# The input of the last SSM quarter is loaded into the tile of a rotation table

## The chip, the cores and the metric

The kernel runs on one core of a Trainium2 chip. The metric is the device time of one execution in microseconds (us), lower is better. The engines of the core are TensorE (PE, matrix products; PEld is its weight load), VectorE (DVE), ScalarE (ACT), GpSimd (POOL) and SyncE (SP, which here only starts transfers, DMAs). Each engine works through its own queue of instructions in order, and waits on semaphores for the other engines and for DMAs.

## What is computed

One layer of a hybrid streaming encoder on 1024 tokens of width 1024, with 16 learned tokens ahead of them. A normed input feeds two mixers side by side, an attention with forgetting and a state-space model (SSM); their outputs are gated and added, projected, and followed by a convolutional feed-forward part. Cut to what matters here:

```python
xn = rmsnorm(h, norm_mix_g)
q, k, v, f_logit, u, gates = split(xn @ w_in)
y_a = forgetting_attention(q, k, v, f_logit) @ w_attn_out
z = gelu(s5(u, ...))                       # s5: x_t = lam_bar * x_{t-1} + B u_t;  y_t = Re(C x_t) + D u_t
zg = z @ w_glu
y_s = zg[..., :1024] * sigmoid(zg[..., 1024:])
g = sigmoid(gates)
h = h + (g[..., :1024] * y_a + g[..., 1024:] * y_s) @ w_o
h = h + conv_ffn(rmsnorm(h, norm_ffn_g))
out = rmsnorm(h, norm_final_g)
```

The SSM has 32 groups of 16 channels, each with 64 complex states.

## The kernel before, in words

**Products.** All large products are done in two parts of reduced precision: each operand is split in a high part (a cast, on ACT or POOL) and a low part (the rest, a subtraction, most on DVE by the helper at line 137, `split_lo`), and three products are added: high by high, low by high, high by low. Weights come in chunks through the pool `wstream` (tile `raw`, two buffers; `whi` and `wlo`, two each). PSUM is taken in banks of 512 columns: three buffers `mm`, one `po`, two `sp`, two `tp`. `mm` and `po` are handed out in turn, so a product's bank is needed again four products later.

**The SSM** (function `ssm`) goes by four quarters of 8 groups. Time is folded in chunks of 8, which leaves 130 chunks. The quarter's input, `u_d[q]` in DRAM, is loaded as the tile `U` (128 x 8 x 130 floats). A quarter q runs in three steps, written as the generator `chain(q)`:

1. the load of `U` (two buffers, so that of quarter 3 takes the place of that of quarter 1), then 16 small products of `U` by the table `Wi`, into `wr` and `wi` (lines 1930 to 1934)
2. the rotation on DVE: `wr` and `wi` times the rotation table (`rc`, `rs`), a scan over the chunks, and the rotation back, into the states `St` (helper line 1653, scans 1951 and 1952). The rotation table is built once for quarters 0 and 1 (`rotation(0)`, tile `pc` in the pool `ssmb`), and once for quarters 2 and 3 (`rotation(1)`, a tile under the tag `pd` in another pool)
3. products of `St` by `Gm` and of `U` by `Tm` (lines 1971 and 1973), the copy to `Y`, a GELU, and the store of `Y` to `y_d[q]` in DRAM.

So `U` is read twice, in step 1 and at the end of step 3. `Wi` is made by `input_tables(q)`, `Gm` and `Tm` by `output_tables(q)`: products into `Kt` (line 1893), copied by ACT (1895), then eight DMAs on SP from `Kt` to `Tm` (1903).

**Around the SSM.** In the same stretch PE has the products for the gates as its main work (`stage_gates`, 8 chunks of 72 products of 342 columns, lines 170 to 172); the SSM's small products are put between them. After the last quarter come the logits of the forget gate (`fg`, lines 537 to 544), the first q and k products (`project_qk(0)`, lines 600 to 610: three blocks for q, three for k, each evicted by casts on ACT and `split_lo` on DVE), and then the GLU, `z @ w_glu`.

**The input of the GLU.** `load_z` loads the four `y_d[m]` as tiles `zt` of 128 x 8 x 130 floats. Each is eight DMAs of 16 partitions (line 641; half of those of m = 3 are started by POOL, the others by SP). They are split in high and low part (`zh`, `zl`, line 646 and the helper), and combined by additions and subtractions into four forms `zf` (lines 661 to 664), which are split too (`z1h`, `z1l` and so on). The GLU is a product by seven half-size products instead of eight (`seven`, lines 232 to 246), so it needs these combinations of its operands. The `zt` tiles, and the GLU's tiles after them, lie in memory that the SSM's pools have given back; a tile that comes to lie where an older one lay waits for the last reader of the older one. The SP queue also carries the loads of the GLU's weights (`raw<-in_w_glu_dram`, line 678), two DMAs for a chunk, into the two `raw` buffers; a load waits until ACT has cast what was in the buffer before (line 154 for the weights of q and k).

**What sets the order.** The code is written step by step, but the order in which instructions stand in each engine's queue is set when the program is built, by the framework's scheduler, which goes by its own estimate of when operands and places are free. The queue is then fixed. The lines at which the quarters are stepped (before, line 566 on):

```python
    begin(1)
    for q in range(4):
        next(chains[q])                                 # step 2 of quarter q
        if q < 3:
            ssm_out(q + 1, sx if q == 1 else None)      # Gm, Tm of the next quarter
        advance(q)                                      # products of the gates
        run(chains[q])                                  # step 3
        if q < 2:
            begin(q + 2)                                # Wi, U, step 1 of quarter q + 2
```

Of the kernel before, what the change touches and what calls it, by code (L numbers as in the profile page):

```python
# [9 lines left out]
F = mybir.dt.float32  # L10
# [9 lines left out]
P = 128  # L20
# [18 lines left out]
NCH = L // CH  # L39
GQ = G // 4  # L40
# [18 lines left out]
def block_kernel(ctx, tc, x, meta, xbt, x0t, g1t, w_q, w_k, w_v, w_f, w_u, w_g, b_f, w_ao, lam_d, bw_d, cw_d,  # L59
# [5 lines left out]
    V, S, GP, PE, SY = nc.vector, nc.scalar, nc.gpsimd, nc.tensor, nc.sync  # L65
# [41 lines left out]
    u_d = dp.tile([SW // P, P, P // GC, NCH], F, name="u_d")  # L107
# [69 lines left out]
    def run(gen):  # L177
        for _ in gen:
            pass
# [113 lines left out]
    sp = ByTag(sb, Gm=sa, Tm=sa, **{tag: sc for tag in ("wr", "wi", "ta", "tb", "dt8", "pd")})  # L293
# [14 lines left out]
    ssm_log, ssm_outs, ssm_loads, ssm_steps = ssm(tc, after, sp, sio, st_ps, ident, u_d, y_d, lam_d, bw_d, cw_d, d_sk, l_dt)  # L308
# [28 lines left out]
    for i in range(5, 9):  # L337
        load_x(i)
    us2, ul2 = (sp.tile([P, 2, n, SW if n == 2 else NCH], dt, tag=tag, name=nm, bufs=1)
                for n, dt, tag, nm in ((CH, F, "pd", "usb"), (2, R, "pc", "ul")))  # L340
    ul = [sio.tile([P, 2, SW], R, tag="U", name="ul", bufs=2) for _ in range(2)] + [ul2[:, i] for i in range(2)]

# [114 lines left out]
        after(ld, queue[-1])  # L457
    next(ssm_steps)
    after(ssm_log[n_log], ready)
    ssm_in, ssm_out, ssm_chain = next(ssm_steps)  # L460


    chains = {}
# [1 line left out]
    def begin(q):  # L465
        ssm_in(q)
        chains[q] = ssm_chain(q)
        next(chains[q])
# [53 lines left out]
    def advance(q):  # L522
        while n_gate[0] < BEHIND[q]:
            next(gates)
            n_gate[0] += 1
# [41 lines left out]
    begin(1)  # L567
    for q in range(4):
        next(chains[q])
        if q < 3:  # L570
            ssm_out(q + 1, sx if q == 1 else None)
        advance(q)
        run(chains[q])
        if q < 2:
            begin(q + 2)
        if q == 1:
            next(ssm_steps)
# [682 lines left out]
    for p in (0, 4, 1, 5, 2, 3, 6):  # L1260
        if p == 2:
# [7 lines left out]
            early = {m: pair_weights(m) for m in (NFF, 0)}  # L1269
# [372 lines left out]
def ssm(tc, after, sp, sio, s_ps, ident, u_d, y_d, lam_d, bw_d, cw_d, d_sk, l_dt):  # L1642
    nc = tc.nc
    V, S, GP, PE, SY = nc.vector, nc.scalar, nc.gpsimd, nc.tensor, nc.sync
# [7 lines left out]
    def TT(*a):  # L1652
        log.append(V.tensor_tensor(*a))
# [4 lines left out]

    bufs = dict(Gm=2, Tm=2, Wi=2, U=2, tq=3, sy=3, wr=2, wi=2, dt8=1, ta=1, tb=1, pc=1, pd=1, dg=1)

    def big(tag, shape, name=None):
        return (sio if tag in ("sy", "U") else sp).tile(shape, F, tag=tag, name=name or tag, bufs=bufs[tag])

# [18 lines left out]
    def rest():  # L1682
# [140 lines left out]
        def rotation(h):  # L1823
            pc = big("pd" if h else "pc", [P, 2, NH, NCH], "pc")
            GP.memset(pc[:, 0, :, 0:1], 1.0)
            GP.memset(pc[:, 1, :, 0:1], 0.0)
            rt = big("sy", [P, 2, 2, NH * 32], "rt")
            m_ = 1
            while m_ < NCH:
                w_ = min(m_, NCH - m_)  # L1830
                lg = m_.bit_length() - 1
                nh = min(NH, NH * 32 // w_)
                t, u = (rt[:, i, :, :nh * w_].rearrange("p c (a w) -> p c a w", w=w_) for i in range(2))
                for a0 in range(0, NH, nh):
                    sl = slice(a0, a0 + nh)
                    br, bi = (eq[lg][:, i, NH * h + a0:NH * h + a0 + nh].unsqueeze(1).unsqueeze(3)
                              .broadcast_to([P, 2, nh, w_]) for i in range(2))
                    times(pc[:, :, sl, m_:m_ + w_], pc[:, :, sl, :w_], br, bi, t, u)
                m_ *= 2
            return pc[:, 0], pc[:, 1]  # L1840
# [65 lines left out]
        def input_tables(qt):  # L1906
# [11 lines left out]
                S.copy(Wi[:, 4 * q:4 * q + 4].rearrange("p g m -> p (g m)"), wt)  # L1918
            state[qt] = [Wi]

        def chain(qt):
            Wi, = state[qt]
            U = big("U", [P, GQ, NCH])
            (S if qt > 1 else SY).dma_start(U, u_d[qt])
            wr, wi = (big(n, [P, HQ, NCH]) for n in ("wr", "wi"))
            for e in range(2):
                for q in range(0, HQ, 2):
                    wps = s_ps()
                    for i in range(2):
                        PE.matmul(wps[:, NCH * i:NCH * i + NCH], Wi[:, 2 * (q + i) + e, :], U[:, 2 * (q + i) + e, :],  # L1930
                                  start=True, stop=True)
                    w3 = wps[:, :NCH * 2].rearrange("p (i n) -> p i n", n=NCH)
                    S.copy(wr[64 * e:64 * e + 64, q:q + 2], w3[:64])
                    S.copy(wi[64 * e:64 * e + 64, q:q + 2], w3[64:])
            yield
            dt8 = big("dt8", [P, HQ, NCH])
            S.copy(dt8, dec[:, qt * HQ:qt * HQ + HQ].unsqueeze(2).broadcast_to([P, HQ, NCH]))
            GP.memset(dt8[:, :, 0:1], 0.0)
            rc, rs = (t_[:, qt % 2 * HQ:qt % 2 * HQ + HQ] for t_ in rot[qt // 2])
            ta, tb = (big(n, [P, HQ, NCH]) for n in ("ta", "tb"))  # L1940
            TT(ta, wr, rc, ALU.mult)
            TT(tb, wi, rs, ALU.mult)
            TT(ta, ta, tb, ALU.add)
            TT(tb, wr, rs, ALU.mult)
            TT(wi, wi, rc, ALU.mult)
            TT(wi, wi, tb, ALU.subtract)

            def fl(t_):
                return t_.rearrange("p a n -> p (a n)")

            V.tensor_tensor_scan(fl(wr), fl(dt8), fl(ta), 0.0, ALU.mult, ALU.add)
            V.tensor_tensor_scan(fl(ta), fl(dt8), fl(wi), 0.0, ALU.mult, ALU.add)
            St = big("sy", [P, GQ, NCH], "St")
            V.memset(St[:, :, 0:1], 0.0)
            S4 = St.rearrange("p (a b) n -> p a b n", b=2)
            for part, (op, fa, fb) in enumerate(((ALU.subtract, wr, ta), (ALU.add, ta, wr))):
                x_, y_ = (tb, wi) if part == 0 else (ta, wr)
                TT(x_, rc, fa, ALU.mult)
                TT(y_, rs, fb, ALU.mult)
                for e in range(2):  # L1960
                    r_ = slice(64 * e, 64 * e + 64)
                    TT(S4[64 * part:64 * part + 64, :, e, 1:], x_[r_, :, :NCH - 1], y_[r_, :, :NCH - 1], op)
            yield
            _, Gm, Tm = state.pop(qt)
            Y = big("sy", [P, GQ, NCH], "Y")
            for q in range(0, GQ, 3):
                nq = min(3, GQ - q)
                yps = s_ps()
                for i in range(nq):
                    yo = yps[:, NCH * i:NCH * i + NCH]  # L1970
                    PE.matmul(yo, Gm[:, q + i, 1:, :].rearrange("p t c -> p (t c)"), St[:, q + i, :],
                              start=True, stop=False)
                    PE.matmul(yo, Tm[:, q + i, :], U[:, q + i, :], start=False, stop=True)
                S.copy(Y[:, q:q + nq].rearrange("p a n -> p (a n)"), yps[:, :NCH * nq])
            outs.append(S.activation(Y, Y, AF.Gelu_apprx_tanh))
            outs.append(GP.dma_start(y_d[qt], Y))

        yield input_tables, output_tables, chain
        rot.append(rotation(1))
        yield  # L1980

    return log, outs, loads, rest()


# [56 lines left out]
```

## Time and profile before

| | |
|---|---|
| time, median of 3 runs | 1444.85 us (1443.14 to 1447.14) |
| the profiled execution: time, span in the profile | 1444.9 us, 1443.1 us |
| busy over the span: PE, PEld | 1422.4 us (99%), 1346.8 us (93%) |
| busy: DVE, ACT, POOL | 1073.0 us (74%), 722.2 us (50%), 762.9 us (53%) |
| mean granted clock of PE | 0.998 |
| SSM quarters, first product of step 1 to last product of step 3 | 87.8 to 180.4 us |
| first product of the GLU | 211.0 us |

The page gives busy times of the engines over the whole span; the views by window, the groups by line, the waits and the timeline go into one stretch. In a timeline row stand the start, the duration, the engine, the line, the operation, out<-in and the shape, and in brackets how long the engine had been idle before it and what ended that. `SPq`, `ACTq` are DMAs started from the queues of SP and ACT. Matmuls overlap each other, so a row's duration is longer than the distance to the next. The time outside the span is 1444.9 less 1443.1, 1.8 us.

### The profile page before, as it was taken

The page shows a single profiled execution, that of the slowest core. Times are in us where ns is not written, and L with a number is a line of the kernel's source. Part 1 is how long each engine was busy: PE and PEld are TensorE (multiplying, and loading weights), DVE is VectorE, ACT ScalarE, POOL GpSimd, SP SyncE. Part 2 cuts the span into 40 slices and gives each one's busy share as a digit, 9 for nine tenths or more (in the row PEclk, how much of TensorE's full clock was granted, in tenths as well). Part 3 has the DMA queues.
Part 4 walks back from the last instruction along what each step waited for, and adds up shares of the span by engine and source line. Part 5 has one row for each costly group of instructions (what it writes and reads, how often), then busy time and mean ns, then how long its engine had stood idle before and what let it go on. Part 6 is the DMA issues. An engine that isn't in the chain of part 4 may idle for free.

```text
span 1443.1 us, 26612 instructions
## 1 busy us (share of the span) xinstructions
PE 1422.4 (99%) x9655; PEld 1346.8 (93%) x9655; DVE 1073.0 (74%) x2203; ACT 722.2 (50%) x1419; POOL 762.9 (53%) x887
## 2 busy tenths in 40 slices
PE   8999999999999999999999999999999999999997
PEld 8999999988999999999879999999999999888886
DVE  7999788843657676656469987788877876788857
ACT  7646585423656565533646544444434445644433
POOL 1542248632456556515871335555555545888794
PEclk9999999999999999999999999999999999999999
DMA  8676644530147422167964156667753327864433
GB/s 303 169 182 164 153 102 151 150 106 30 38 130 165 126 66 67 45 222 244 267 147 142 63 139 170 171 164 190 187 136 116 92 71 262 328 204 142 123 87 117
DMA packets 92968, 214.06 MB, mean 148 GB/s; under 512 B 15090, under 2 KB 22898, under 8 KB 92452
## 3 DMA queue, kind: packets, MB, share of 16 engines
q1 hardware_dynamic: 73124, 166.32, 35.2%
q0 software_dynamic: 17696, 41.29, 15.2%
q10 hardware_dynamic: 2016, 4.74, 0.9%
q8 instruction: 76, 1.25, 0.4%
q14 instruction: 56, 0.46, 0.1%
HBM read 170.88 MB, written 71.71 MB: 168 GB/s over the span
## 4 chain that ended last, share of the span: by engine, by line
PE 91%; DVE 5%; DMA 1%; ACT 1%; issue 1%; POOL 0%; SPq 0%; POOLq 0%; ACTq 0%; DVEq 0%
PE mm L172 5%; PE mm L170 5%; PE mm L171 5%; PE sp L232 4%; PE sp L233 4%; PE sp L234 4%; PE tp L232 3%; PE tp L233 3%; PE tp L234 3%; PE mm L232 3%; PE mm L234 3%; PE mm L233 3%; PE tp L860 3%; PE mm L1557 2%; PE mm L1555 2%; PE mm L1556 2%
## 5 line engine op out<-in xcount | busy, mean ns | idle before, releaser
L170 PE MATMUL mm<-xhi,whi 128*128 128x342 f32 (+2 forms) x480 | 156.8, 327 | 1.0 <-DVE q L137 1.0
L172 PE MATMUL mm<-xhi,wlo 128*128 128x342 f32 (+2 forms) x480 | 155.3, 324 | 0.0
L171 PE MATMUL mm<-xlo,whi 128*128 128x342 f32 (+2 forms) x480 | 155.2, 324 | 0.0
L1183 POOL TENSOR_TENSOR ov<-ov,og 128x1024 f32<-128x1024 f32 x21 | 50.8, 2421 | 117.1 <-ACT og L1182 114.7
L137 DVE TENSOR_TENSOR sw<-sf,sw 128x512 fp32r<-128x512 f32 x72 | 73.5, 1021 | 45.6 <-ACT sw L1174 45.3
L1174 ACT CAST sw<-sf 128x512 fp32r<-128x512 f32 x72 | 44.9, 623 | 111.3 <-POOL sf L1321 82.3
L170 PEld LDWEIGHTS mm<-xhi,whi 128*128 128x128 f32 x480 | 90.5, 188 | 2.1 <-PE sp L818 0.8
L172 PEld LDWEIGHTS mm<-xhi,wlo 128*128 128x128 f32 x480 | 90.2, 188 | 0.6 <-issue 0.2
L171 PEld LDWEIGHTS mm<-xlo,whi 128*128 128x128 f32 x480 | 90.4, 188 | 0.2
L867 ACT CAST th<-tp 128x256 fp32r<-128x256 f32 (+3 forms) x120 | 56.1, 471 | 62.5 <-PE tp L860 30.2
L137 DVE TENSOR_TENSOR tl<-tp,th 128x256 fp32r<-128x256 f32 (+3 forms) x120 | 65.2, 547 | 25.9 <-ACT th L867 24.5
L1321 POOL TENSOR_TENSOR sf<-raw,sf 128x512 f32<-128x512 f32 x36 | 63.5, 1764 | 38.7 <-DVE sw L137 38.6
L1321 POOL TENSOR_TENSOR sf<-raw 128x512 f32<-128x512 f32 x36 | 49.1, 1364 | 62.2 <-ACT sw L1174 22.2
L234 PE MATMUL mm<-xhi,sw 128*128 128x258 f32 (+1 forms) x288 | 81.0, 281 | 0.0
L232 PE MATMUL mm<-xhi,sw 128*128 128x258 f32 (+1 forms) x288 | 80.8, 281 | 0.0
L233 PE MATMUL mm<-xlo,sw 128*128 128x258 f32 (+1 forms) x288 | 80.7, 280 | 0.0
L832 POOL TENSOR_SCALAR pt<-pt,nm 128x144 f32<-128x144 f32 (+4 forms) x72 | 52.1, 736 | 49.9 <-DVE nm L831 48.9
L1373 DVE SCALAR_TENSOR_TENSOR ov<-hv,cwt,ov 128x1024 f32<-128x1024 f32 x36 | 68.5, 1904 | 0.4 <-ACT ov L1371 0.4
L1174 ACT CAST sw<-raw 128x512 fp32r<-128x512 f32 x70 | 43.0, 620 | 46.6 <-PE sp L234 22.6
L830 ACT ACTIVATE pt<-pt,nm 128x144 f32<-128x144 f32 (+4 forms) x72 | 52.9, 735 | 25.7 <-DVE nm L829 25.2
L137 DVE TENSOR_TENSOR sw<-raw,sw 128x512 fp32r<-128x512 f32 x70 | 58.3, 837 | 5.3 <-ACT sw L1174 5.1
L823 DVE CUSTOM_DVE_ANT_0 pt<-sp,fb 128x328 f32<-128x328 f32 (+8 forms) x112 | 46.4, 430 | 21.2 <-PE sp L818 12.6
(722 smaller groups left out, 5720.7 us busy)
## 6 DMA issues: line engine op xcount, KB each, us to landing
raw<-in_w_up_dram SPq DMA_DIRECT2D x44, 512.0 KB, 3.8
t_d<-in_w_dn_dram POOLq DMA_DIRECT2D x44, 256.0 KB, 6.7
wr<-t_d SPq DMA_DIRECT2D x44, 256.0 KB, 3.8
ar<-a_d SPq DMA_DIRECT2D x41, 256.0 KB, 5.2
a_d<-ov SPq DMA_DIRECT2D x18, 512.0 KB, 2.6
wr<-in_w_dn_dram SPq DMA_DIRECT2D x33, 256.0 KB, 4.0
t_d<-in_w_dn_dram SPq DMA_DIRECT2D x22, 256.0 KB, 4.7
t_d<-t_d SPq DMA_DIRECT2D x22, 256.0 KB, 4.6
```

The lines of the kernel that those rows point to most:

```text
L137: return eng.tensor_tensor(out_, src, hi.bitcast(F), ALU.subtract)
L170: yield PE.matmul(ps, whi[:, i, :], ahi[:, i], start=(i == 0), stop=False)
L171: yield PE.matmul(ps, whi[:, i, :], alo[:, i], start=False, stop=False)
L172: yield PE.matmul(ps, wlo[:, i, :], ahi[:, i], start=False, stop=(i == k - 1))
L232: PE.matmul(ps, a[0][:, i], bh, start=(i == 0 and not joins), stop=False, skip_group_check=True)
L233: PE.matmul(ps, a[0][:, i], bl, start=False, stop=False, skip_group_check=True)
L234: PE.matmul(ps, a[1][:, i], bh, start=False, stop=(i == kh - 1), skip_group_check=True)
L830: S.activation(pt[:n, :kc], pt[:n, :kc], AF.Exp, bias=nm[:n, 1:2], scale=0.125, accum_out=nm[:n, 2:3])
L867: S.copy(th[:kn, z:tw], tp[:kn, z:tw])
L1174: S.copy(hi, src)
L1321: sums.append(GP.tensor_tensor(f_, a, b, op))
L1373: V.scalar_tensor_tensor(out=o, in0=h_[:, j:SEQ + j], scalar=cwc(j, m), in1=o, op0=ALU.mult, op1=ALU.add)
```

## The change

The load of `U` is taken out of `chain` into a function of its own, `load_u`. For quarter 3 the tile is no longer a buffer of the tag `U`: it is allocated under the tag `pc`, in the place of the rotation table of quarters 0 and 1. And the load of quarter 3 is called earlier in the code, right behind step 2 of quarter 1 instead of at the start of step 1 of quarter 3. It is still started from the ACT queue. Nothing else in the text changes.

```diff
@@ the stepping of the quarters
     begin(1)
     for q in range(4):
         next(chains[q])
+        if q == 1:
+            ssm_u(3)
         if q < 3:
             ssm_out(q + 1, sx if q == 1 else None)
         advance(q)
@@ in ssm
+        early = {}
+
+        def load_u(qt):
+            U = sp.tile([P, GQ, NCH], F, tag="pc", name="U", bufs=1) if qt == 3 else big("U", [P, GQ, NCH])
+            (S if qt > 1 else SY).dma_start(U, u_d[qt])
+            early[qt] = U
+            return U
+
         def chain(qt):
             Wi, = state[qt]
-            U = big("U", [P, GQ, NCH])
-            (S if qt > 1 else SY).dma_start(U, u_d[qt])
+            U = early.pop(qt) if qt in early else load_u(qt)
             wr, wi = (big(n, [P, HQ, NCH]) for n in ("wr", "wi"))
...
-        yield input_tables, output_tables, chain
+        yield input_tables, output_tables, chain, load_u
```

(`ssm_u` is `load_u` as the stepping code names it.) Behind the inserted lines the line numbers of the changed kernel are higher by 2, and behind `load_u` by 9.

The scheduler makes a new order of it, and three places of it matter below. The first is the ACT queue around step 1 of quarter 2, whose copies are `wr` and `wi`, and step 3 of quarter 1, whose copies are `Y`. Before:

```order
L1933 COPY wr<-tp 64x260
L1934 COPY wi<-tp 64x260
L1933 COPY wr<-sp 64x260
L1934 COPY wi<-sp 64x260
L1895 COPY Kt<-tp 16x512
...
L1974 COPY Y<-tp 128x260
L1924 DMA U<-u_d 128x1040
L1975 ACT_TABLE_LOAD
```

and now:

```order
L1942 COPY wr<-tp 64x260
L1943 COPY wi<-tp 64x260
L1927 DMA U<-u_d 128x1040
L1942 COPY wr<-sp 64x260
L1943 COPY wi<-sp 64x260
L1897 COPY Kt<-tp 16x512
...
L1983 COPY Y<-tp 128x260
L1984 ACT_TABLE_LOAD
```

The load of quarter 3 stands ahead of the last two copies of step 1 of quarter 2, where it stood behind the last copy of `Y` of quarter 1.

The second place is the SP queue behind the last DMA to `Tm`. Before:

```order
L1903 DMA Tm<-Kt 16x8x16
L641 DMA zt<-y_d 16x8x130 x16
L678 DMA raw<-in_w_glu_dram 128x512 x2
L641 DMA zt<-y_d 16x8x130 x8
L678 DMA raw<-in_w_glu_dram 128x512 x2
L641 DMA zt<-y_d 16x8x130 x4
L675 DMA gl<-g_d 128x1026 x2
```

and now:

```order
L1905 DMA Tm<-Kt 16x8x16
L680 DMA raw<-in_w_glu_dram 128x512 x4
L643 DMA zt<-y_d 16x8x130 x28
L677 DMA gl<-g_d 128x1026 x2
L680 DMA raw<-in_w_glu_dram 128x512 x4
```

The weights of the first two GLU chunks stood behind the first 16 and behind 24 of the 28 loads of `zt`; now both pairs stand ahead of all 28.

The third place is the DVE queue while PE does the q and k products: `q` and `kl` are the evictions of these, `zl`, `z2l`, `z3l` and `zf` work on the GLU's input, `ops` on its weights, `fg` on the forget gate. Before:

```order
L663 TENSOR_TENSOR zf<-zt,zf 128x8x65
L137 TENSOR_TENSOR q_2517<-po,q_2517 64x272
L137 TENSOR_TENSOR q_2518<-po,q_2518 64x272
L664 TENSOR_TENSOR zf<-zt,zf 128x8x65
L137 TENSOR_TENSOR zl_2435<-zt,zh_2434 128x8x130
L549 SCALAR_TENSOR_TENSOR fg<-fg 40x520
L137 TENSOR_TENSOR z2l<-zf,z2h 128x520
L137 TENSOR_TENSOR z3l<-zf,z3h 128x520
L137 TENSOR_TENSOR zl_2433<-zf,zh_2432 128x520
L137 TENSOR_TENSOR q_2517<-mm,q_2517 64x384
L137 TENSOR_TENSOR q_2518<-mm,q_2518 64x384
```

and now, from the same place behind the first block of q:

```order
L665 TENSOR_TENSOR zf<-zt,zf 128x8x65
L666 TENSOR_TENSOR zf<-zt,zf 128x8x65
L137 TENSOR_TENSOR zl_2435<-zt,zh_2434 128x8x130
L137 TENSOR_TENSOR z2l<-zf,z2h 128x520
L137 TENSOR_TENSOR z3l<-zf,z3h 128x520
L137 TENSOR_TENSOR zl_2433<-zf,zh_2432 128x520
L663 TENSOR_TENSOR zf<-zt 128x8x65
L137 TENSOR_TENSOR q_2517<-mm,q_2517 64x384
L137 TENSOR_TENSOR q_2518<-mm,q_2518 64x384
L137 TENSOR_TENSOR zl_2435<-zt,zh_2434 128x8x130
L549 SCALAR_TENSOR_TENSOR fg<-fg 40x520
L665 TENSOR_TENSOR zf<-zt,zf 128x8x65
```

with these behind them:

```order
L137 TENSOR_TENSOR z1l<-zf,z1h 128x520
L137 TENSOR_TENSOR ops<-raw,ops 128x256
L137 TENSOR_TENSOR ops<-sf,ops 128x256
L137 TENSOR_TENSOR q_2517<-mm,q_2517 64x384
L137 TENSOR_TENSOR q_2518<-mm,q_2518 64x384
L137 TENSOR_TENSOR ops<-raw,ops 128x256
L137 TENSOR_TENSOR ops<-sf,ops 128x256
L137 TENSOR_TENSOR z3l<-zf,z3h 128x520
L666 TENSOR_TENSOR zf<-zt,zf 128x8x65
L137 TENSOR_TENSOR kl<-mm,k_2519 64x272
L137 TENSOR_TENSOR kl<-mm,k_2520 64x272
```

The first split of a `zt` into `zl` and most of the work on `zf` stood ahead of the evictions of q; now the work on the third and fourth `zt` stands between the evictions of the first, second and third block of q. The queues of POOL and ACT have the work on `zt` later in the same way. On PE one piece moves: the products of `U` by `Wi` of quarter 3, and those into `Kt`, stand 17 gate products earlier.

More of the change, by code (lines that the diff above doesn't have):

```diff
@@ L459, in block_kernel @@
     after(ssm_log[n_log], ready)
-    ssm_in, ssm_out, ssm_chain = next(ssm_steps)
+    ssm_in, ssm_out, ssm_chain, ssm_u = next(ssm_steps)
     chains = {}
```

## Prediction

> **What bounds the kernel now.** I read the page's first part first.
>
> ```profile
> PE 1422.4 (99%) x9655; PEld 1346.8 (93%) x9655; DVE 1073.0 (74%) x2203; ACT 722.2 (50%) x1419; POOL 762.9 (53%) x887
> ```
>
> PE is busy for 99% of the span, so an edit off PE gains only where it ends a wait of PE. The view of PE's waits shows what there is to gain.
>
> ```profile
> PE mm L351 <- ACT uh L409: 5.0, 1, 5.0
> ...
> PE sp L1930 <- DMA U<-u_d: 1.1, 1, 1.1
> ```
>
> The first row belongs to the start of the program. The second is the only wait that this edit can touch: step 1 of quarter 3 waits for its input. The chain of waits and PE's timeline show it in place (start, duration; in brackets the idle time before the row).
>
> ```profile
> 133.63 9.33 DMA U<-u_d
> ...
> 145.12 0.16 PE mm L170
> ```
>
> ```profile
> 143.10 0.68 PE L1930 MATMUL sp<-U,Wi 128*128 128x130 f32 x4 [1.11 <-DMA U<-u_d]
> ...
> 180.27 0.39 PE L1973 MATMUL tp<-U,Tm 128*128 128x130 f32 x2
> ```
>
> The transfer takes 9.33 us, and PE stands still for the last 1.11. The last product of `U` by `Tm`, the last reader of the tile, starts at 180.27; that matters below.
>
> **What is gained.** The old place of `U` is free long before 133.63, and only the instruction's position on ACT held the load back. In the new place it waits for the last read of `pc` by the rotation of quarter 1 on DVE, and ACT waits with it.
>
> ```profile
> 126.61 0.70 DVE L1653 TENSOR_TENSOR ta<-pc,ta 128x520 f32<-128x520 f32 x1
> ...
> 145.98 0.70 DVE L1653 TENSOR_TENSOR ta<-wr,pc 128x520 f32<-128x520 f32 x1
> ```
>
> ```profile
> 126.31 0.37 ACT L1933 COPY wr<-sp 64x260 f32<-64x260 f32 x1
> ...
> 128.51 0.57 ACT L1895 COPY Kt<-tp 16x512 f32<-16x512 f32 x1 [1.45 <-PE tp L1893]
> ```
>
> That read ends at 126.61 + 0.70 = 127.31. Without the DMA, the third copy of step 1 starts at 126.31, so ACT stands for about 1.0, then issues (0.4; SP's last row below has 1.75 / 4 = 0.44 for one). Behind it stand the two copies of 0.37 each, which end at 127.3 + 0.4 + 0.75 = 128.5 instead of 127.1, and then the copy of `Kt` at 128.51, which waited 1.45 for PE anyway. DVE reads what these copies write from 145.98. So the new wait costs nothing; without that cover it would cost PE up to 1.3.
>
> The load is then issued at 127.3 to 127.7 and, at 9.33, lands by 137.0. PE was free for it at 143.10 - 1.11 = 142.0, and now comes to it 17 gate products earlier, at 0.16 each (the second row of the chain): 142.0 - 2.7 = 139.3. The transfer would have to take 11.7 to be late. **Gain: 1.1 us**, and all of PE's later work comes 1.1 earlier.
>
> **What is lost.** In the old place nothing followed `U`. The new one lies where the `zt` tiles of m = 1 and m = 2 are put afterwards, so these two loads get a wait for the last `U` by `Tm` product of quarter 3 (180.27, now about 179.2). That wait itself is met in time, as the next numbers show. But the scheduler, going by its own estimates, turned the SP queue round for it: all four loads of GLU weights now stand ahead of all 28 loads of `zt`. This is what costs. SP before:
>
> ```profile
> 155.44 10.35 SPq L641 DMA_DIRECT2D zt<-y_d  x16
> 165.90 0.90 SPq L678 DMA_DIRECT2D raw<-in_w_glu_dram  x2
> ...
> 174.87 4.92 SPq L641 DMA_DIRECT2D zt<-y_d  x8
> 179.95 0.83 SPq L678 DMA_DIRECT2D raw<-in_w_glu_dram  x2
> ...
> 189.94 1.75 SPq L641 DMA_DIRECT2D zt<-y_d  x4
> ```
>
> Before, 16 loads of `zt` were started from 155.44. The second pair of `raw`, at 179.95, could not go earlier than its buffer came free, and that is by ACT's cast of the weights of k:
>
> ```profile
> 176.96 1.05 ACT L154 CAST whi<-raw 128x1024 fp32r<-128x1024 f32 x1 [0.88 <-PE po L171]
> ```
>
> It ends at 178.01, was waiting for PE (0.88), and so comes 1.1 earlier: 176.9. Now this wait stands ahead of every `zt`, and behind it on SP stand the 28 loads and then the loads of `gl`. With 0.90 for the pair the first `zt` starts at **177.8**, 22 us later than before. The wait for 179.2 falls on m = 1, whose turn comes after eight loads, at 177.8 + 8 x 0.65 = 183.0, so it costs nothing.
>
> 24 loads (m = 0, 1, 2) take 10.35 + 4.92 = 15.27, so the last of m = 2 is issued at 193.1. From issue to use:
>
> ```profile
> 182.46 1.27 DVE L663 TENSOR_TENSOR zf<-zt,zf 128x520 f32<-128x520 f32 x1 [6.15 <-DMA raw<-in_w_glu_dram]
> ...
> 186.48 1.83 DVE L137 TENSOR_TENSOR z2l<-zf,z2h 128x520 fp32r<-128x520 f32 x1
> ...
> 196.24 1.29 DVE L663 TENSOR_TENSOR zf<-zt,zf 128x520 f32<-128x520 f32 x1 [0.83 <-DMA zt<-y_d]
> ```
>
> ```profile
> 186.17 1.59 POOL L662 TENSOR_TENSOR zf<-zt 128x520 f32<-128x520 f32 x1
> 190.21 2.16 POOL L641 DMA_DIRECT2D zt<-y_d  x4 [2.45 <-DMA y_d<-Y]
> ...
> 196.35 2.38 POOL L662 TENSOR_TENSOR zf<-zt 128x520 f32<-128x520 f32 x1 [0.43 <-issue]
> ```
>
> The loads issued until 174.87 + 4.92 = 179.79 were used by DVE at 182.46, 2.67 later (the row names the weights, but no operand of it is one). The last four of SP, issued until 191.69, and of POOL, until 192.37, were used from 196.24: at most 4.5 and 3.9. I take 3.2, near the first. So the work on m = 2 begins at 193.1 + 3.2 = **196.3**. Before, that was the time of m = 3 (the rows at 182.46 and 186.48 are of m = 2); now DVE and ACT have both ahead of, and between, the evictions of q and k. The four loads of m = 3, 1.75 behind m = 2, are there before either engine comes to them. What DVE then has to do, and when PE needed the banks:
>
> ```profile
> 197.56 0.89 DVE L137 TENSOR_TENSOR q<-po,q 64x272 fp32r<-64x272 f32 x2
> 198.49 1.37 DVE L664 TENSOR_TENSOR zf<-zt,zf 128x520 f32<-128x520 f32 x1
> 199.75 2.39 DVE L137 TENSOR_TENSOR zl<-zt,zh 128x1040 fp32r<-128x1040 f32 x1
> ...
> 203.79 0.68 DVE L137 TENSOR_TENSOR zl<-zf,zh 128x520 fp32r<-128x520 f32 x1
> 204.49 1.12 DVE L137 TENSOR_TENSOR q<-mm,q 64x384 fp32r<-64x384 f32 x2
> 205.64 0.42 DVE L137 TENSOR_TENSOR ops<-raw,ops 128x256 fp32r<-128x256 f32 x1
> ...
> 208.36 0.89 DVE L137 TENSOR_TENSOR kl<-mm,k 64x272 fp32r<-64x272 f32 x2
> ```
>
> ```profile
> 206.76 0.34 PE L170 MATMUL mm<-xhi,whi 128*128 128x384 f32 x1
> ...
> 211.00 0.28 PE L232 MATMUL mm<-zh,ops 128*128 128x260 f32 x1
> ...
> 211.72 0.28 PE L232 MATMUL mm<-zh,ops 128*128 128x260 f32 x1
> ```
>
> From 196.24 to 204.49 ten instructions took 8.25; their durations add up to 1.29 + 0.89 + 1.37 + 2.39 + 4 x 0.68 = 8.66 (four small ones, the last at 203.79), since rows overlap. So I take 0.953 of a sum. By the order now, and by these rows:
>
> - From 196.3 to the eviction of the second block of q: two `zf` 1.29 + 1.37, `zl` 2.39, three splits 3 x 0.68, `zf` 1.27, the eviction 1.12: 9.48, by 0.953 9.0, done at 205.3. The third product block of k takes that bank, at 206.76 - 1.1 = 205.65. No stall, with 0.3 to spare.
> - To the eviction of the third block of q: `zl` 2.39, `fg` 0.68, `zf` 1.29, `z1l` 0.68, two `ops` 0.84, the eviction 1.12: 7.00 more, 15.7 in all, done at 212.0. The first product of the GLU needs that bank at 211.00 - 1.1 = 209.9. **Stall 2.1.**
> - To the eviction of the first block of k: two `ops` 0.84, `z3l` 0.68, `zf` 1.37, `kl` 0.89: 3.78 more, 19.3 in all, done at 215.6. The second bank of the GLU needs it at 211.72 - 1.1 + 2.1 = 212.7. **Stall 2.9.**
>
> ACT has the like in its own queue:
>
> ```profile
> 196.18 2.36 ACT L646 CAST zh<-zt 128x1040 fp32r<-128x1040 f32 x1 [3.08 <-DMA zt<-y_d]
> ...
> 199.88 0.63 ACT L668 CAST zh<-zf 128x520 fp32r<-128x520 f32 x1 [0.39 <-DVE zf L664]
> 200.54 0.48 ACT L600 CAST q<-mm 64x384 fp32r<-64x384 f32 x1
> ...
> 201.53 0.41 ACT L682 CAST ops<-raw 128x256 fp32r<-128x256 f32 x1
> ...
> 204.00 0.38 ACT L605 CAST k<-mm 64x272 fp32r<-64x272 f32 x1
> ...
> 215.04 0.65 ACT L241 COPY c<-mm 128x260 f32<-128x260 f32 x2
> ```
>
> ```profile
> 215.47 0.39 PE L232 MATMUL mm<-zh,ops 128*128 128x260 f32 x1
> ```
>
> From 196.3 to the casts of the first block of k stand two casts `zh` of a `zt` (2 x 2.36), five of a `zf` (5 x 0.63), four of q (4 x 0.48) and four `ops` (4 x 0.41): 11.4. From there to the copy `c` it was 215.04 - 204.00 = 11.04 without a pause that new work could fill, and two more casts of a `zf`, 0.63 each, now stand in it: 12.3. So `c` starts at 220.0. The product at 215.47 followed its start by 0.43: 220.45, against 215.47 - 1.1 + 2.1 + 2.9 = 219.35. **Stall 1.1.**
>
> Before, PE was idle ahead of none of these four products (no brackets). Behind them I see nothing on DVE, ACT or POOL by which PE could win time back, since PE has no waits there to give up; so a stall reaches the end whole.
>
> **The sum.** -1.1 + 2.1 + 2.9 + 1.1 = +5.0. On the profiled execution's 1444.9 (span 1443.1 and 1.8 around it) this is **1449.9 us**. That execution lies on the median of the runs, 1444.85, so nothing is to be shifted.
>
> **Bounds.** The start of the work on m = 2 is the unknown. Its early end: the loads go at the pace of the last four, 1.75 / 4 = 0.44, and are used 2.67 later: 177.8 + 10.5 + 2.7 = 191.0. Then DVE is in time everywhere (206.7 against 209.9, 210.3 against 210.6), ACT is late by 0.8, and the net is -0.3: 1444.6. Its late end: 16 loads at 0.647 as at 155.44, and 4.5: 197.8, 1.5 later, which gives stalls of 1.2, 2.4, 2.9 and 1.1, net +6.5: 1451.4. The other unknown is how DVE and POOL get on. At 186.48 DVE's `z2l` took 1.83 where its like took 0.68, while POOL ran a `zf` of 1.59 from 186.17. Two such additions of POOL, those for m = 2 and m = 3, now fall in DVE's busiest stretch; at 1.15 each this adds up to 2.3, so the upper end is 1453.7. I take none of it in the sum, since beside the like addition of POOL at 196.35 it was POOL that took longer (2.38), and DVE's rows from 196.24 on kept to within 0.1 of 1.27.
>
> [...]
>
> **The rivals.**
>
> - *The loads are quick and the work on `zt` stays hidden; only the wait of `U` goes.* For it: the four loads at 189.94 went at 0.44. Against it: the 24 ahead of them at 0.61 to 0.65, with the same size. It decides at 196.3 - 6.1 = 190.2, that is 24 loads at (190.2 - 2.7 - 177.8) / 24 = 0.40 each. Time 1444.9 - 1.1 = 1443.8; with 0.44 it is 1444.6. Chance 0.18.
> - *DVE and POOL block each other (as the row 186.48), and PE waits longer.* For it that row; against it the rows from 196.24 on, which kept their usual durations. Time 1449.9 + 2.3 = 1452.2, with late loads 1453.7 and above. Chance 0.13.
> - *The change doesn't do what it says:* the load of `U`, now beside other traffic, takes over 11.7, and PE waits as before. Against it: 9.33 with traffic of its own at 133.95. Then the losses stand without the gain: 1451.0. Chance 0.03.
>
> **How the numbers follow.** The forecast has 0.66, with 1444.6 to 1451.4 as its own range. A measurement of this kernel tells 0.3% from no change, 4.3 us: faster is below 1440.5, which no case reaches, since the gain is at most 1.1; I leave it 0.02. Slower is above 1449.2. The sum lies just above that; of the forecast I put a little over half there (0.35), with nearly all of the two heavier rivals (0.15): 0.50, and 0.48 for no change. The range goes from the first rival, 1443.6, to 1454.0, beyond the upper bound.
>
> **What would show it.** Right: PE's row of waits for `U` is gone, and the load's start is near 127.5; ACT waits there for a read of `pc`; SP starts the first `zt` near 178 behind `raw`; the first `zf` of m = 2 on DVE starts near 196; PE waits before the first GLU products for DVE's `q` and `kl`, then for ACT's `c`, 2 to 3 us each. Wrong: the work on m = 2 begins before 192, or PE's waits between 205 and 221 add up to less than 3 us, or waits of a microsecond follow in the later chunks of the GLU, which I have at nothing.

## The result, and the profile after

The changed kernel takes 1453.03 us (median of 6 runs, 1451.53 to 1456.66), the kernel before 1444.65 (6 runs, 1443.14 to 1447.14): a ratio of 1.006, with a 95% interval of 1.0047 to 1.0073. It is 8.4 us slower, where 5.0 were forecast. The profiled execution of the changed kernel is the longest of its six (span 1454.9).

PE's waits between 100 and 300 us, where the change lies (line waited for: us in total, times, longest):

```profile
PE mm L170 <- DVE q L137: 3.5, 1, 3.5
PE mm L232 <- DVE kl L137: 2.9, 1, 2.9
```

The wait for `U` is gone. In its place stand two waits for evictions by DVE, 3.5 for the second block of q and 2.9 for the first block of k.

The gain first. ACT and PE around the early load, from the timeline:

```profile
126.85 0.33 ACTq L1927 DMA_DIRECT2D U<-u_d  x1
127.22 0.37 ACT L1942 COPY wr<-sp 64x260 f32<-64x260 f32 x1 [1.42 <-DVE ta L1655]
...
128.02 0.57 ACT L1897 COPY Kt<-tp 16x512 f32<-16x512 f32 x1
```

```profile
138.68 0.61 PE L1939 MATMUL sp<-U,Wi 128*128 128x130 f32 x4
```

ACT stands 1.42 for the last read of `pc`, as foreseen, and the copy of `Kt` takes the delay up: it has no idle time left before it. `U` is issued at 126.85, and PE comes to it at 138.68 without a wait.

Then the loss. SP, and DVE and POOL behind it:

```profile
161.28 15.68 SPq L680 DMA_DIRECT2D raw<-in_w_glu_dram  x4
177.08 18.50 SPq L643 DMA_DIRECT2D zt<-y_d  x28
```

```profile
198.47 1.31 DVE L665 TENSOR_TENSOR zf<-zt,zf 128x520 f32<-128x520 f32 x1 [4.12 <-DMA zt<-y_d]
199.82 2.30 DVE L666 TENSOR_TENSOR zf<-zt,zf 128x520 f32<-128x520 f32 x1
...
207.25 1.12 DVE L137 TENSOR_TENSOR q<-mm,q 64x384 fp32r<-64x384 f32 x2
...
217.52 0.89 DVE L137 TENSOR_TENSOR kl<-mm,k 64x272 fp32r<-64x272 f32 x2
```

```profile
198.63 2.31 POOL L664 TENSOR_TENSOR zf<-zt 128x520 f32<-128x520 f32 x1 [6.28 <-DMA zt<-y_d]
```

The row of `raw` spans the wait of its second pair; the first `zt` goes at 177.08. The work on m = 2 begins at 198.47, where 196.3 was forecast. The second `zf` on DVE takes 2.30 beside POOL's of 2.31; before it took 1.37. So the evictions come at 207.25 and 217.52, and PE behind them:

```profile
208.52 0.48 PE L170 MATMUL mm<-xhi,whi 128*128 128x384 f32 x1 [3.47 <-DVE q L137]
...
214.70 0.36 PE L232 MATMUL mm<-zh,ops 128*128 128x260 f32 x1 [0.19 <-DVE q L137]
...
218.56 0.36 PE L232 MATMUL mm<-zh,ops 128*128 128x260 f32 x1 [2.90 <-DVE kl L137]
```

These are the products that began at 206.76, 211.00 and 211.72 before. PE was ready for the first of them at 208.52 - 3.47 = 205.05, which is 1.7 earlier than before: so large is the gain where the first wait begins. 1.1 of it is the wait for `U`. Another 0.5 was there already at the first product of `U` by `Tm`, in quarter 0 (110.5 against 111.0), ahead of the new load; a wait of 0.3 for DVE between 100 and 110 is part of it, which the changed kernel's profile doesn't have. Whether the change brings that part isn't shown. Waits of 6.6 less a gain of 1.7 make 4.9, and the kernel lost 8.4. The rest is in the view of windows. Its columns are the stretch, its length, the busy time of PE, PEld, DVE, ACT and POOL (instructions in brackets), and then the granted clock of PE; the stretches are steps of 3.41 us counted from the changes of that clock (208.68, 212.09, 218.92 and 222.33):

```profile
205.27:208.68 3.41, 0.16 (x1) 0.19 (x2) 3.33 (x6) 1.76 (x5) 1.90 (x1) 1.00 0.00 0
208.68:212.09 3.41, 3.41 (x12) 3.41 (x12) 3.41 (x4) 3.31 (x9) 0.00 (x0) 0.50 0.47 154
212.09:215.51 3.42, 3.23 (x20) 2.88 (x18) 3.36 (x9) 3.35 (x6) 0.09 (x1) 0.99 0.00 0
215.51:218.92 3.41, 0.51 (x5) 0.39 (x4) 3.33 (x5) 3.36 (x6) 2.50 (x2) 1.00 0.08 14
218.92:222.33 3.41, 3.41 (x18) 3.41 (x18) 3.33 (x6) 3.35 (x9) 2.64 (x3) 0.50 0.42 144
```

Behind each of the two long waits, of 3.47 and 2.90, PE was granted half its clock (0.50) for 3.41 us. It did 12 products in 208.68 to 212.09, and 20, some of them smaller, in the next stretch. By an estimate from these rows, a clock of 0.50 for 3.41 us, each such stretch cost 3.41 / 2 = 1.7 us. The sum is 3.5 + 0.2 + 2.9 + 2 x 1.7 = 10.0, less the gain of 1.7: 8.3. The products of `wvh` by `xhi`, behind all of this, show the same (first and last start), before and after:

```profile
L754 PE MATMUL mm<-wvh,xhi x48: 387/393/497, 292.4 to 334.6; 128*128 128x512 f32 x48
```

```profile
L756 PE MATMUL mm<-wvh,xhi x48: 387/392/505, 301.1 to 343.3; 128*128 128x512 f32 x48
```

They start 8.7 us later, which agrees with the medians. The profiled execution is 11.8 longer in span. The rest, 3.1, belongs to a wait near 1320 and one more stretch of half clock behind it, 1.8 + 1.7 = 3.5:

```profile
PE sp L1557 <- DVE hs L1567: 1.8, 1, 1.8
```

```profile
1318.01:1321.43 3.42, 1.59 (x8) 1.24 (x7) 3.42 (x6) 2.28 (x4) 2.79 (x3) 1.00 0.45 152
1321.43:1324.84 3.41, 3.41 (x10) 2.63 (x9) 3.41 (x5) 0.00 (x0) 2.15 (x3) 0.50 0.43 146
```

A row of DVE ahead of it, at 1310.34, took 6.02 beside rows of POOL; in the kernel before no single row of that group took over 1.78 there. The prediction has no term for this wait. The profiles of three runs below have it too (1.7 or 1.8; the place alone, the order put back, the places exchanged), and the others don't. In the run with the place alone the clock behind it stayed at 1.00. Whether the change brings it isn't shown.

### The profile page after: what moved, and what is told of

Same layout as the page of the kernel before. It is cut to its first block, busy times and chain, and to the rows that moved or that the text cites. A ratio compares the mean times of both kernels' runs of the same rounds, so it can differ in the third digit from the quotient of the medians.

```text
span 1454.9 us, 26612 instructions
## 1 busy us (share of the span) xinstructions
PE 1427.7 (98%) x9655; PEld 1350.6 (93%) x9655; DVE 1069.8 (74%) x2203; ACT 722.3 (50%) x1419; POOL 758.9 (52%) x887
## 4 chain that ended last, share of the span: by engine, by line
PE 93%; DVE 2%; issue 2%; DMA 1%; ACT 1%; SPq 0%; POOL 0%; POOLq 0%; DVEq 0%; ACTq 0%
PE mm L170 5%; PE mm L172 5%; PE mm L171 5%; PE sp L233 4%; PE sp L232 4%; PE sp L234 4%; PE mm L232 3%; PE mm L234 3%; PE tp L232 3%; PE tp L233 3%; PE tp L234 3%; PE mm L233 3%; PE tp L862 3%; PE mm L1559 2%; PE mm L1558 2%; PE mm L1557 2%
```

## The experiments

The questions: do late data make the waits, or the new order of the queues, or the place of `U`? And is the half clock the price of any long wait of PE, or something of this place? Each new median stands beside one of the kernel before that was measured along with it. The diffs show the lines that matter, and some are written shorter than they are. Several expectations put the gain at 1.8, between the 1.7 above and the 1.9 by which the last product of `U` by `Tm` came earlier (178.5 against 180.4).

**The order of SP alone, on the kernel before.** `U` stays where and when it was.

```diff
         for q in range(2):
-            SY.dma_start(raw[:, 4 * q:4 * q + 4], w_glu[KD * q + i])
+            ld = SY.dma_start(raw[:, 4 * q:4 * q + 4], w_glu[KD * q + i])
+            for zl_ in zt_ld if i < 2 else []:      # all loads of zt
+                after(zl_, ld)
```

> The kernel before, U in its old place and loaded at its old time; only the SP queue is tied to the order of the changed kernel: all four loads of GLU weights ahead of the 28 loads of zt (DVE, ACT and POOL then get the work on zt late too). Theory (the late start of the zt loads costs, not the new place of U): no gain on U, so PE comes to the evictions 1.8 us later than in the changed kernel, and so do the weights of k and the loads; the work on m = 2 starts near 200.3, PE waits for DVE's q and kl for about 6.5 us in all, and half clock after the long waits costs 3.4 more: 1444.7 + 10 = 1454.7 (1452 to 1457). Rival (the place of U itself, by its waits on SP and ACT, costs): no loss here, 1444.7.

Measured: 1454.74 us against 1445.92, ratio 1.0067 (1.0052 to 1.0082). PE's waits:

```profile
PE mm L170 <- DVE q L137: 5.4, 1, 5.4
PE mm L232 <- ACT c L241: 1.4, 1, 1.4
PE mm L232 <- DVE kl L137: 0.9, 1, 0.9
```

The waits add up to 7.7, and behind the first the clock was 0.50 and 0.51 for two stretches (207.37 to 214.20), in the first of which PE was busy for 0.16 of 3.42 us. So the place of `U` as such isn't needed for the loss: it comes with late loads of `zt`, and the queues that go with them, in a kernel that keeps `U` where it was.

**The place alone.** The early call is taken back, the place kept.

```diff
         next(chains[q])
-        if q == 1:
-            ssm_u(3)
         if q < 3:
```

> The new place of U for quarter 3 alone; the call that loads it stands in the code where it stood before, at the start of step 1 of quarter 3. The scheduler makes the same queues of it as of the whole change. Theory (the place, not the line of the call, decides): the time of the changed kernel, 1453.0 (1451.5 to 1454.5), the load still started near 127. Rival (the early call matters): U lands late again, and PE's wait for it is back.

Measured: 1454.22 us against 1444.22, ratio 1.0062 (1.0047 to 1.0078).

```profile
126.83 0.33 ACTq L1925 DMA_DIRECT2D U<-u_d  x1
```

The load goes at 126.83 with the call where it was, and PE waits 4.0 for q and 2.8 for `kl`. The line of the call decides nothing here; the place gives both the early load and the loss.

**The order of SP put back, on the changed kernel.**

```diff
+            if i < 2:
+                after(ld, zt_ld[(15, 23)[i]])
+                for zl_ in zt_ld[(16, 24)[i]:]:
+                    after(zl_, ld)
```

> The changed kernel with the SP queue tied to the order of before (16 zt, 2 weights, 8 zt, 2 weights, 4 zt); U stays in the place of pc, so the loads of m = 1 and everything behind them on SP wait for the last product of U, near 179. DVE and ACT keep their late order of the work on zt, with small differences. Theory: m = 0 is loaded from 155, m = 1 from 179, m = 2 issued until about 190.5 and landed near 194 to 196 instead of 198.5, so the waits of PE shrink from 6.5 to 2 to 4 us, with one half-clock stretch or none: 1446 to 1450. Rival (order of the SP queue was the only cause): all of the loss goes, 1442.9.

Measured: 1453.22 us against 1445.92, ratio 1.0053 (1.0036 to 1.007): 7.3 us slower, where the changed kernel is 8.4, a difference within the intervals. The expectation failed, and so did its rival.

```profile
151.17 32.50 SPq L645 DMA_DIRECT2D zt<-y_d  x16
```

```profile
195.49 1.36 DVE L667 TENSOR_TENSOR zf<-zt,zf 128x520 f32<-128x520 f32 x1 [2.49 <-DMA zt<-y_d]
...
213.56 0.89 DVE L137 TENSOR_TENSOR kl<-mm,k 64x272 fp32r<-64x272 f32 x2
```

The work on m = 2 began 3.0 us earlier than in the changed kernel, and the wait for q went. But in this order more work on m = 3 stands ahead of `kl`: it came at 213.56, PE waited 4.3 for it and 0.9 for ACT's `c`, and had half clock for two stretches of 3.41 (0.51 and 0.50, 213.38 to 220.21).

**The places of m = 1 and m = 3 exchanged.** The same, with the tiles taken in the order 0, 3, 2, 1.

```diff
-        for m in range(4):
-            tag = "gl" if m % 2 else "ms"
-            zt = gz[tag].tile([P, CH, NCH], F, tag=tag, name="zt", bufs=2)
+        for m in (0, 3, 2, 1):
+            tag = "gl" if m % 2 else "ms"
+            places[m] = gz[tag].tile([P, CH, NCH], F, tag=tag, name="zt", bufs=2)
```

> As the run with the order of SP put back, and the tiles of zt of m = 1 and m = 3 exchange their places, so that only m = 2 and m = 3 lie over the new place of U. The loads of m = 0 and 1 go at 155, those of m = 2 at about 179 to 184.5, landed near 188. Theory (late data make the waits): DVE is in time for all evictions (188 + 19.3 = 207.3 against 209.2), no wait of PE, no half clock, and the gain of 1.8 is left: 1442.9. Rival (the order on DVE, with the work on zt between the evictions of q and k, costs by itself even when the data are there): PE waits of 2 us or more before the GLU, 1445 or above.

Measured: 1451.71 us against 1445.92, ratio 1.0048 (1.0033 to 1.0063). The edit did not do what it was meant to: the loads of m = 1 still waited, since the 16 loads span as long as above:

```profile
151.24 32.46 SPq L648 DMA_DIRECT2D zt<-y_d  x16
```

So this run repeats the one before it and tells nothing of the question.

**Early data, late order.** The pools are laid in another order, so that only m = 2 (and `zf`) lies over `U`; SP is tied as above.

```diff
-    gz = {n: pool(st_k2, "gated" + n, side="left") for n in ("ms", "gl", "cg")}
+    gz = {n: pool(st_k2, "gated" + n, side="left") for n in ("ms", "cg", "gl")}
```

> U stays in the place of pc as in the changed kernel. The pools of the gated tiles are laid in another order, so that only the zt of m = 2 (and zf) lie over U, and the SP queue is tied to the order of before. The loads of m = 0 and 1 go from 151, those of m = 2 from 179. DVE, ACT and POOL keep the late order that they have in the run with the order of SP put back (work on zt between the evictions of q and k). Theory (late data make the waits, the order alone does not): work on m = 2 can begin near 189 to 190, PE waits for less than 1 us, no half clock: 1443 to 1444. Rival (the order on DVE and ACT costs by itself): PE waits 2 us or more in front of the GLU, with half clock behind it: 1446 or above.

Measured: 1448.35 us against 1444.96, ratio 1.0017 (1.0007 to 1.0027). Here the edit did what it was meant to: m = 1 no longer waits for `U`, and the loads of m = 2 begin at 178.67.

```profile
150.73 12.19 SPq L645 DMA_DIRECT2D zt<-y_d  x16
```

```profile
190.96 2.12 DVE L667 TENSOR_TENSOR zf<-zt,zf 128x520 f32<-128x520 f32 x1
...
206.50 0.72 DVE L549 SCALAR_TENSOR_TENSOR fg<-fg 40x520 f32<-40x520 f32 x1
```

```profile
PE tp L232 <- ACT ops L690: 2.1, 1, 2.1
```

```profile
207.30 1.28 ACT L552 ACT_TABLE_LOAD   x1 [2.02 <-DVE fg L549]
```

With the work on m = 2 begun 7.5 us earlier (190.96 against 198.47) DVE is in time for q and, but for 0.2, for `kl`. So that part of the loss is late data. But the order costs too: the forget gate's step at 206.50 (201.96 before) stands on DVE behind the work on m = 3, ACT stood 2.02 for it, and `ops` behind it on ACT came late. PE waited 2.1, again with half clock (0.50) behind, here for two stretches:

```profile
215.32:218.73 3.41, 2.97 (x13) 2.63 (x13) 3.33 (x5) 3.30 (x10) 2.88 (x4) 0.50 0.58 191
218.73:222.15 3.42, 3.42 (x17) 3.42 (x17) 2.51 (x6) 1.43 (x6) 2.48 (x5) 0.50 0.44 154
222.15:225.56 3.41, 3.41 (x31) 3.41 (x30) 2.98 (x7) 2.09 (x4) 1.86 (x3) 1.00 0.04 5
```

**The price of a wait.** Far from the change, DVE multiplies a tile by 1.0 in place, as often as `HOLD` says, ahead of an eviction.

```diff
+        for _ in range(HOLD.get(n_seven[0], 0)):
+            hold = V.tensor_scalar(bot[:, last], bot[:, last], 1.0, None, ALU.mult)
         for q in st:
-            add(bot[:, q["l"]], prod(q, "b", None, A22, T4), q["c1"])
+            ev = add(bot[:, q["l"]], prod(q, "b", None, A22, T4), q["c1"])
+            if hold is not None:
+                after(ev, hold)
```

> The kernel before with PE made to wait in the feed-forward products, far from the change: in six of the 16 doubled blocks DVE gets 12, 16, 20, 24, 28 and 32 extra products by 1.0 in place, ahead of an eviction that PE needs. Theory: each wait of PE of about 3 us or more is followed by a stretch of 3.4 us at half the granted clock, which costs PE 1.7 us more; waits under 1 us are followed by none. Rival (the half clock in the changed kernel came from something else at that place, such as its other engines or DMAs): the clock stays at 1.00 through waits of any length.

> As the run with extra products on DVE in the feed-forward part, but fewer of them: 6, 7, 8, 9, 10, 10 and 11 in seven of the doubled blocks, for waits of PE of some 0.5 to 2.5 us. Theory, from the run before this: the clock is set for stretches of 3.41 us by the stretch before; where PE stood still for more than about half of a stretch (1.7 us or more that fall into one), the next is at half clock, so waits under 1.4 bring none and waits of 2 and more bring one where they fall into one stretch. Rival (any wait of a microsecond or more does, or only waits near 3 us): half clock after waits of 1.0 to 1.4, or none at all after waits of 2.0 to 2.5.

The first of these runs, one execution of 1490.81 us, has waits of 2.72, 5.34, 6.00, 7.38 and 8.09, and half clock behind each: its mean granted clock is 0.985, where the runs of the kernel before beside it have 0.997 or 0.998. The shortest wait, in windows:

```profile
949.37:952.78 3.41, 1.15 (x9) 1.15 (x10) 3.07 (x8) 2.73 (x4) 0.00 (x0) 1.00 0.04 6
952.78:956.19 3.41, 3.41 (x19) 3.41 (x17) 1.62 (x2) 0.66 (x2) 0.00 (x0) 0.51 0.00 0
```

The second, one execution of 1463.87 us, has waits of 0.82, 0.83, 1.31, 1.73 and 2.31, and half clock behind the longest alone; its mean granted clock is 0.996. Here are that one, and the wait of 1.31, which falls into one stretch (3.41 - 2.10 = 1.3):

```profile
989.20:992.61 3.41, 1.45 (x12) 1.45 (x13) 3.13 (x6) 1.14 (x1) 1.08 (x1) 1.00 1.07 183
992.61:996.02 3.41, 3.41 (x19) 3.41 (x18) 3.27 (x3) 2.79 (x6) 0.00 (x0) 0.51 0.58 106
...
1074.53:1077.94 3.41, 2.10 (x18) 1.89 (x17) 3.34 (x9) 0.00 (x0) 1.49 (x2) 1.00 0.90 130
1077.94:1081.36 3.42, 3.42 (x29) 3.42 (x30) 3.04 (x5) 3.25 (x5) 0.00 (x0) 1.00 0.19 36
```

So in these runs half clock came behind waits far from the changed place, and nothing of that place is needed for it. The stretches shown with PE busy for 1.15 and 1.45 us at full clock had a clock of 0.51 in the next; the one with 2.10 kept 1.00. The theory's "about half" was the author's estimate: these stretches only leave room for it, between 1.45 and 2.10 us, and show no such line.

**The table moved to another pool.** The new place of `U` is kept off all `zt`.

```diff
-    sp = ByTag(sb, Gm=sa, Tm=sa, **{tag: sc for tag in ("wr", "wi", "ta", "tb", "dt8", "pd")})
+    sp = ByTag(sb, Gm=sa, Tm=sa, **{tag: sc for tag in ("pc", "wr", "wi", "ta", "tb", "dt8", "pd")})
```

> The changed kernel, but the rotation table of quarters 0 and 1, and with it the new place of U, lies in another pool: in that of wr, wi, ta and tb, which the z tiles cover, and no zt. SP has the order of before again (16 zt, 2 weights, 8 zt, 2 weights, 4 zt), PE the early products of U of the changed kernel, DVE and ACT the order of before but for a few rows. Theory (what costs is that the zt lie over the pool that U now keeps open, and that the queues are ordered for that): no wait of PE before the GLU, no half clock, and the gain of 1.8 us is left: 1442.9. Rival (the early load itself, or PE's earlier products, bring the waits): 1446 or more.

Measured: 1446.99 us against 1444.96, ratio 1.001 (0.9998 to 1.0021): no difference that is clear of the measurement, and not the 1442.9 expected.

```profile
PE mm L170 <- DVE fg L544: 2.9, 1, 2.9
```

```profile
184.14 1.22 DVE L665 TENSOR_TENSOR zf<-zt,zf 128x520 f32<-128x520 f32 x1 [13.90 <-DMA raw<-in_w_glu_dram]
...
191.57 0.48 DVE L544 SCALAR_TENSOR_TENSOR fg<-mm,bf,fg 8x272 f32<-8x272 f32 x1
```

The waits for q and `kl` are gone. But the eviction of the forget gate (191.57; 188.84 before) stands behind work that waits for m = 2 (the row names the weights, but no operand of it is one), and PE, which comes earlier now, waits 2.9 for it, with half clock (0.51) for 3.42 behind it (193.30 to 196.72).

**That eviction put ahead.**

```diff
             z_ = V.tensor_tensor(f2, part(1, 1, k), f1, ALU.subtract)
+            if k == 0:
+                for x_ in fg_v[:2]:       # the first two evictions of fg
+                    after(z_, x_)
```

(and the same for their copies on ACT)

> As the run with the table moved to another pool, and on DVE and ACT the first two evictions of the forget gate (fg) are tied ahead of the work on zf of k = 0 that needs m = 2. Theory (in that run PE waited 2.9 us for fg only because fg stood behind a zf that waits for the load of m = 2): this wait and its half clock go, no wait of over 0.5 us stands between 100 and 300 us, and the gain of 1.8 us is left: 1442.9 to 1443.4. Rival (the load of m = 2 sets the time of the whole stretch, so PE meets the next wait behind it): some wait of 1 us or more shows between 190 and 215, 1444.5 or above.

Measured: 1448.08 us against 1444.22, ratio 1.0023 (1.0014 to 1.0031).

```profile
PE mm L232 <- ACT c L241: 1.4, 1, 1.4
PE tp L232 <- ACT ops L693: 1.0, 1, 1.0
PE mm L170 <- DVE q L137: 0.8, 1, 0.8
```

The wait for `fg` is gone, and three others stand behind it, 3.2 in all, which is more than the gain. None of them brought half clock (the granted clock is 1.00 from 180 to 300), and the profiled execution is 2.0 longer in span than that of the kernel before. The rival was right.

**Only PE's order.** On the kernel before, the products of `U` by `Wi` of quarter 3 are tied behind nine more gate products.

```diff
             g_ = next(gates)
             n_gate[0] += 1
+            if 409 <= n_gate[0] <= 417:
+                for mm_ in u_first:       # U by Wi of quarter 3
+                    after(mm_, g_)
```

> The kernel before, U in its old place and loaded at its old time; the products of U by Wi of quarter 3 are tied behind nine more products of the gates on PE, 1.4 us of work. Theory (the wait of 1.1 us for U is all that the old load costs): the wait goes, 1.1 to 1.3 us faster: 1443.4, with nothing else moved. Rival (the later step 1 makes the rotation of quarter 3 late and the time comes back there): 1444.7.

Measured: 1444.65 us against 1444.96, ratio 0.9998 (0.9988 to 1.0008).

```profile
PE mm L170 <- DVE fg L548: 1.1, 1, 1.1
```

PE's wait for `U` is gone, and this one has come, as long as that which went. It looks as if the wait had moved: the forget gate's eviction, which stands behind work on m = 2, has no room for a PE that comes earlier. But this is one execution. That of the run with the shorter waits above, whose queues up to here have the order of the kernel before, has 0.7 for `U` and 1.8 for `fg`. So a wait for `fg` comes without this edit as well. What the 12 executions show is that nothing was gained.

**The same, with the eviction of fg put ahead,** as two runs above.

> As the run with the products of U by Wi tied later, and with the same first two evictions of fg tied ahead. Theory: the wait of 1.1 us for fg that came back there is gone, and 1.3 to 1.8 us of gain are left: 1443.2. Rival: as above, 1444.5.

Measured: 1451.36 us against 1444.22, ratio 1.0048 (1.0033 to 1.0062).

```profile
PE mm L170 <- DVE fg L550: 2.4, 1, 2.4
```

The tie moved other rows as well, and a later eviction of `fg` came late; 1.4 for ACT's `c` came on top, and the mean granted clock of the profiled execution is 0.995, where that of the kernel before is 0.998. It is 7 us slower than the kernel before, where the run without the tie was level. No version that was run is clearly faster than the kernel before.

## Why the prediction was right, and where it was off

The sign and the mechanism were right. By its steps:

- **The gain** held in its mechanism: 1.1 was taken, and the wait of 1.11 is gone. Its size was short: PE came 1.7 earlier to the first wait, the other 0.6 being outside that wait. The transfer's 9.33 did not matter; in the new place it landed in 3.4. ACT's wait was covered, as worked out.
- **The start of the `zt` loads** held: 177.8 was taken, 177.08 measured. So did the rate: the last of m = 2 was issued by 192.3 (193.1).
- **From issue to use** failed: 3.2 was taken and 6.2 measured, beyond the upper bound of 4.5, so that the work on m = 2 began at 198.5. The row taken as nearest, 2.67, belonged to a run of eight loads. The view of DMA issues has the median from issue to landing (the last number): of those eight, and then, in the changed kernel, of the loads in 177 to 182, in 182 to 187.5, and in 187.5 to 192.8, which hold m = 2:

```profile
zt<-y_d SPq DMA_DIRECT2D x8, 65.0 KB, 3.0
```

```profile
zt<-y_d SPq DMA_DIRECT2D x9, 65.0 KB, 6.1
```

```profile
zt<-y_d SPq DMA_DIRECT2D x7, 65.0 KB, 3.6
```

```profile
zt<-y_d SPq DMA_DIRECT2D x12, 65.0 KB, 5.4
```

  So the length of the run alone doesn't give the time, which doesn't grow along it. But the kernel before showed more than 2.67 as well: its 16 loads from 155.44 have a median of 4.3, the safer row to take.
- **The stall for the second block of q** was taken at nothing, with 0.3 to spare, and measured 3.5: the 2.2 us of late start, 0.9 by DVE's `zf` beside POOL's (2.30 for 1.37), which the sum left out as a bound, and 0.6 by the larger gain, less the 0.3. The stall for the third block, taken at 2.1, came out at 0.2, since the first stall and the half clock behind it (3.5 + 1.7) had already given DVE its time. That for `kl` was taken at 2.9 and measured 2.9. ACT's `c`, taken at 1.1, cost nothing here. Of 6.1 forecast, 6.6 came, with other shares: their sum was right by luck as much as by working.
- **"So a stall reaches the end whole"** failed, and it is the largest miss: two stalls brought two stretches of half clock, 3.4 us that no term of the sum held. With them, with 6.6 of stalls for 6.1 and with 1.7 of gain for 1.1, the 5.0 becomes 8.3.
- **The rival with DVE and POOL** (1452.2) comes nearest in time, but only 0.9 of its 2.3 came, by DVE's `zf` of 2.30 beside POOL's of 2.31 (1.37 before); that the two block each other isn't shown beyond such rows. The measured 1453.0 lies beyond the sum's own late end, 1451.4, and within the stated range only by the room left for this rival. The half clock filled that room, which is luck.
- **The rival of hidden work** (1443.8) was tried by the runs with the data early: even then the order of the queues, and PE's own earlier arrival, brought other waits.
- That a stall is the only price of the new place was assumed, and the run with the product tied later suggests a further thing that the prediction missed, though one execution doesn't show it: the gain itself would have met the wait for `fg`, had the scheduler not taken the work on m = 2 out of its way.
- Two slips changed no forecast: from 196.24 to 204.49 stand nine instructions of DVE, not ten (the 8.66 is right), and the range's lower end, 1443.6, is not quite the 1443.8 of the rival that it is taken from.

What stays open: why the 28 loads landed so late (other transfers ran beside them, and no run took them away), where 0.6 of the gain comes from, whether the wait near 1320 belongs to the change, and by which estimate the scheduler ordered the queues; its orders are read from the queues alone.

## What to carry to other kernels

When a tile moves to a place that lies under later tiles, cost the order that the scheduler makes of it, not only the wait that it takes away: here 1.1 us were won and 28 loads went 22 us later. A wait of an engine that sets the time is worth no more than the slack of the next wait behind it, which is read from the rows behind it. And a long stall of PE had a second price here: behind waits of 2.1, 2.31, 2.72, 2.90 and 3.47 us the clock was 0.50 or 0.51 for 3.41 us or twice that, so that one long stall cost more than several short ones: three waits of 1.4, 1.0 and 0.8, 3.2 us in all, brought none, a single one of 2.90 did.

## What the runs showed of the hardware

In the profile of the changed kernel the granted clock was 1.00 or 0.50. Between 100 and 1400 us it changed at 208.68, 212.09, 218.92, 222.33, 1321.43 and 1324.84, each a whole number of steps of 3.41 us behind the one before: 1, 2, 1, 322 (1099.10 / 322 = 3.413) and 1. Of the stretches of one step that were read here, these at full clock were followed by one at half clock: those in which PE was busy for 0.16 and 0.51 us (the changed kernel), 0.35 (the order of SP put back), 1.15 and 1.45 (the two runs with DVE's added products), 1.20 (the table moved), 1.29 (early data) and 1.32 (the order of SP alone). One with 2.10 (1074.53 to 1077.94 in the run with the shorter waits) was followed by full clock. Between these both occur: 1.59 near 1320 in the changed kernel brought half clock, and 1.66 at the same place in the run with the place alone (1317.74 to 1321.15) did not. At half clock, stretches with PE busy for 0.16 us (207.37 to 210.79 in the run with the order of SP alone), 2.19 (213.38 to 216.79 in the run with the order of SP put back) and 2.97 (215.32 to 218.73 in the run with early data) were followed by another at half clock, and ones with 3.14 (216.79 to 220.21 in the run with the order of SP put back) and with 3.41 by full clock. So in these executions 3.41 - 1.45 = 2.0 us of standing still within one stretch were enough, 1.3 were not, and with about 1.8 it went either way.
